# The cross branch's projection computed as four Strassen pairs behind the pairs of the input projection

## The chip, the cores and the metric

The kernel runs on one core of one Trainium2 chip. The metric is the device time of one execution in microseconds (us); the kernel before was timed in three runs. One more execution was profiled, and the durations below come from it. The five engines are called TensorE (PE in the profile, PEld its weight loads), VectorE (DVE), ScalarE (ACT), GpSimd (POOL) and SyncE (SP); SP, ACT and POOL also issue DMA transfers. Each engine executes its own instructions in program order, and waits for other engines through semaphores.

## The reference

One layer of a decoder trunk for 1024 prompt tokens and 8 sample tokens (1032 columns in all), width 1024, in float32. What matters here:

```python
proj = h @ w_in                     # one input projection: q, k, v, gates, u, merge, ...
br_gla = o * jax.nn.silu(gla_g)     # branch 0: gated linear attention
br_pool = p * jax.nn.silu(pool_g)   # branch 1: multi-scale pooling
br_x = c * jax.nn.silu(xg)          # branch 2: cross attention
bproj = einsum('btnw,nwd->btnd', stack([br_gla, br_pool, br_x]), w_branch)
gates = jax.nn.sigmoid(merge)       # one gate per branch and channel
merged = sum(gates * bproj, axis=branch)
y = x + merged @ w_out              # then a final RMSNorm
```

So each of the three branches, 1024 channels by 1032 columns, is multiplied by its own 1024 by 1024 matrix, gated, and summed into one array.

## The kernel before

**Precision.** A float32 value is split into a high half, rounded (ScalarE copy), and the rest (VectorE subtraction), and a product is three matmuls: high by high, high by low and low by high (`split`, lines 221 and 222; `mm3`, lines 240 to 242).

**Input projection.** It runs as 40 *pairs* (class `Pair`). A pair produces 256 output channels for all 1032 columns by one level of Strassen's scheme in Winograd's form: seven products of halves instead of eight. `RIGHT` names the right-hand operands of the products, `11`, `21`, `t2`, `t1`, `t3`, `22`, `t4`: quarters of the input and sums of quarters, 512 channels by 516 columns each. They are split once and stay in SBUF, in 28 tiles of 1032 columns, for all pairs. The left-hand ones (`a11`, `a12`, `s2`, `s1`, `s3`, `s4`, `a22`) are quarters of the pair's weights and sums of them, built anew for each pair by VectorE (`operands`, line 301) and split. One product is 24 matmuls of 258 columns (three per 128 channels of the sum and half of the columns). ScalarE copies partial results out of PSUM (line 612), VectorE adds them (lines 677, 694 and 703).

**Order.** `seq` lists the products: 0 to 4 of a pair, then product 0 of the next pair, then 5 and 6. I write (i, j) for product j of pair i. The weights of a product are prepared three products ahead (`AHEAD`). TensorE's and SP's instructions stand in the order in which the code emits them; those of VectorE, ScalarE and GpSimd are put in order by a scheduler when the kernel is built. Into the pairs a stream of other work is woven (attention, then pooling), which ends before pair 36. Pairs 28 to 39 are *gated*: their result goes through SiLU, is multiplied by a branch's value (`mix`) and stored as the branch's array `br_scr`. Pairs 16 to 27 give the merge gates `m_scr`.

**Branch projection, direct.** After the last pair come 24 *units*: three branches in the order of `ORDER` (cross, GLA, pool), eight blocks of 128 output channels each. `branch_k` loads and splits a branch's array (16 tiles); a unit is 72 matmuls, 24 each for three column blocks of 384, 384 and 264. The result is multiplied by the sigmoid of the merge gate (line 1508), added to the sum so far (line 1510) and stored in `acc_scr`. The output projection follows.

**Buffers.** Wide tiles: `E`, 30 of 1032 columns. Ring tiles: `R`, 15 of 512 columns. Weight halves: `W2`, 8. Raw weights: `RAW`, 3. PSUM: six banks `px` for the products. A load into a wide tile has to wait until the tile's last reader is done.

Of the kernel before, what the change touches and what calls it, by code (L numbers as in the profile page):

```python
# [18 lines left out]
P = 128  # L19
D = 1024  # L20
T = 1024
NS = 8
# [20 lines left out]
EW = 1032  # L43
EXP_LN_SET = 6
# [3 lines left out]
def trunk_kernel(ctx: ExitStack, tc: tile.TileContext,  # L48
# [65 lines left out]
    def R(shape, dt=F32, name="r"):  # L114

        return shaped(wk.tile([P, 512], dt, tag="ring", name=name, bufs=NR), shape)

    def V(shape, dt=F32, name="v"):
        return shaped(wk.tile([P, 512], dt, tag="own", name=name, bufs=4), shape)
# [68 lines left out]
    brs = [cp.tile([P, NK, NS], F32, name=f"brs{n}") for n in range(3)]  # L188
# [13 lines left out]
    acc_scr = [scratch(NK, f"acc{n}_", (P, TT)) for n in range(2)]  # L202
# [78 lines left out]
    ORDER = (2, 0, 1)  # L281

    class Pair:


        def __init__(self, src, dst, s0=None, gated=None, turned=False):
            self.src, self.dst, self.s0, self.gated, self.raw = src, dst, s0, gated, [None, None]
            self.turned = turned
# [300 lines left out]
    def operand(name, k, src):  # L589
        hi, lo = (E([2, HT], F32R, name=f"o{name}{k}{j}") for j in range(2))  # L590
        split(hi, lo, src)
        ops.setdefault(name, []).append((hi, lo))
# [12 lines left out]
    def run_product(n):  # L605
# [18 lines left out]
        def finish(t, e):  # L624
# [3 lines left out]
            if p.gated:  # L628
# [11 lines left out]
                nc.vector.tensor_tensor(t[:, :, 512:HT], t[:, :, 512:HT], ss, op=ALU.mult)  # L640
            if p.turned:
# [24 lines left out]

        if j == 0:
# [13 lines left out]
        elif j == 2:  # L681
            p.r2 = []
            for c in product(p.x, n, False):
                p.r2.append(saved(p.x, c, "r2"))
                yield
# [5 lines left out]
        elif j == 4:  # L691
            for c in product(p.x, n, False):
# [6 lines left out]
        elif j == 5:  # L699
            p.e2 = E([2, HT], name="c2")  # L700
            mixed(1)
            for c in product(p.z, n, False):
# [4 lines left out]
        else:  # L707
            for c in product(p.x, n, False):
# [92 lines left out]
    def cross_scaled(h):  # L801
        xs = wk.tile([P, 16], F32, tag="xsq", name="xsq", bufs=2).rearrange("p (i b) -> p i b", i=2)
# [528 lines left out]
    def emit(n, ahead=AHEAD):  # L1331
        prepare(n + ahead)
        if seq[n] == (28, 0):
# [102 lines left out]
    units = [(o, n, d) for o, n in enumerate(ORDER) for d in range(NK)]  # L1436
    inputs = {}

    def fetch(u):
# [10 lines left out]
        acc = None  # L1450
        if o > 0:
            acc = E([TT], name="acc")
            nc.sync.dma_start(out=acc, in_=acc_scr[o - 1][d])
        inputs[u] = w, sig, acc
# [3 lines left out]
    for n in range(5, len(seq)):  # L1458
        for _ in range({7: 2, 5: 1, 4: 1, 3: 1, 2: 1, 1: 1}.get(len(seq) - n, 0)):
            br.append(branch_k(ORDER[0], len(br)))  # L1460
# [3 lines left out]
    br.append(branch_k(ORDER[0], 7))  # L1464
# [29 lines left out]
    for u, (o, n, d) in enumerate(units):  # L1494
        if d == 0 and o:
# [3 lines left out]
        w, sig, acc = inputs.pop(u)  # L1499
        act(sig, sig, AF.Sigmoid)  # L1500
        ts = [PX() for _ in CH]
# [4 lines left out]
        for t, (c0, cw) in zip(ts, CH):  # L1506
            cs = slice(c0, c0 + cw)
            nc.vector.tensor_tensor(sig[:, cs], t[:, :cw], sig[:, cs], op=ALU.mult)
            if o > 0:
                nc.vector.tensor_tensor(sig[:, cs], acc[:, cs], sig[:, cs], op=ALU.add)  # L1510
        if o < 2:
            nc.gpsimd.dma_start(out=acc_scr[o][d], in_=sig)
# [43 lines left out]
    for hf, order in enumerate(ORDERS):  # L1556
        for tb in order:
# [13 lines left out]
            if hf == 0:  # L1571
                x = (E([D], name="y") if tb < 8 else RAW("ys").rearrange("p a b -> p (a b)"))[:m]
                nc.sync.dma_start(out=x, in_=x_p[tb * P:(tb + 1) * P] if tb < 8 else x_s)
                rows_[tb], sums[tb] = x, wk.tile([P, 4], F32, tag="yq", name="yq", bufs=9)[:m]
# [69 lines left out]
```

## Time and profile before

| | us |
|---|---|
| median of three runs (lowest, highest) | 1431.19 (1431.14, 1432.55) |
| the profiled execution | 1428.62 |
| its span, first to last instruction | 1426.9 |
| TensorE busy | 1403.6 (98%) |
| VectorE busy | 919.8 (64%) |
| ScalarE busy | 678.3 (48%) |
| direct branch projection, first matmul to the output projection's first | 1054.40 to 1326.37 |

The profiled execution is 2.57 us, 0.18%, below the median of the runs; 1.7 us of it lie outside the span. A window row gives, for a stretch of the span, each engine's busy time with its number of instructions, TensorE's granted clock, the share of the 16 DMA engines and the traffic. A timeline row gives start, duration, engine, line, operation and, in brackets, the idle time before it and what ended it. Matmuls overlap, so the busy time of one is longer than the distance to the next.

### The profile page before, as it was taken

How to read it: one execution, taken by the hardware profiler on the slowest of the kernel's cores; microseconds unless marked ns; L12 is line 12 of the kernel's file. 1: busy time of each engine (PE TensorE's matmuls, PEld its weight loads, DVE VectorE, ACT ScalarE, POOL GpSimd, SP SyncE). 2: the span in 40 equal slices, each digit the busy share in tenths (PEclk: the TensorE clock that was granted, in tenths of full speed). 3: DMA queues.
4: the chain of work that ended last, by engine and by line, in shares of the span. 5: the costliest groups of instructions: out<-in, count | busy, mean ns of one | idle time of the engine just before them, and what ended most of it. 6: DMA issues, size and time to landing. Idle time of an engine off the chain costs nothing.

```text
span 1426.9 us, 28403 instructions
## 1 busy us (share of the span) xinstructions
PE 1403.6 (98%) x10625; PEld 1345.0 (94%) x10625; DVE 919.8 (64%) x2108; ACT 678.3 (48%) x1582; POOL 293.6 (21%) x529
## 2 busy tenths in 40 slices
PE   7999999999899999999999999999999999999998
PEld 6899999999899999999999999999999999999876
DVE  6956766857687777767765777876662534654336
ACT  6744434534566656656554545444472422333222
POOL 4154222336442222222221111110000000000000
PEclk9999999999999999999999999999999999999999
DMA  9367786877564565545444556476484687632633
GB/s 347 117 202 248 251 280 208 258 222 237 138 190 130 170 192 163 165 152 166 155 150 146 176 162 210 150 217 204 150 263 148 225 273 232 228 105 86 227 112 117
DMA packets 194197, 270.05 MB, mean 189 GB/s; under 512 B 24252, under 2 KB 144084, under 8 KB 194052
## 3 DMA queue, kind: packets, MB, share of 16 engines
q1 hardware_dynamic: 129692, 151.36, 34.1%
q0 software_dynamic: 26208, 78.94, 15.5%
q10 hardware_dynamic: 38160, 37.95, 9.6%
q8 instruction: 83, 1.36, 0.4%
q14 instruction: 54, 0.44, 0.1%
HBM read 185.84 MB, written 82.80 MB: 188 GB/s over the span
## 4 chain that ended last, share of the span: by engine, by line
PE 92%; DMA 4%; DVE 3%; ACT 1%; issue 1%; SPq 0%; POOL 0%; ACTq 0%; DVEq 0%
PE px L240 26%; PE px L241 26%; PE px L242 26%; PE pz L241 2%; PE pz L242 2%; PE pz L240 2%; DMA raw<-in_w_in_dram 2%; PE pz L461 1%; PE pz L1040 1%; PE pz L1019 1%; DMA qb<-xqs 1%; PE pz L867 1%; PE pz L1021 1%; DMA pT<-pts 0%; PE pz L1126 0%
## 5 line engine op out<-in xcount | busy, mean ns | idle before, releaser
L240 PE MATMUL px<-bh,wbh 128*128 128x384 f32 (+1 forms) x576 | 184.3, 320 | 0.0
L241 PE MATMUL px<-bl,wbh 128*128 128x384 f32 (+1 forms) x576 | 184.0, 319 | 0.0
L242 PE MATMUL px<-bh,wbl 128*128 128x384 f32 (+1 forms) x576 | 183.8, 319 | 0.0
L612 ACT ACTIVATE r<-px 128x258 f32<-128x258 f32 x240 | 90.1, 377 | 54.4 <-PE px L242 53.5
L241 PEld LDWEIGHTS px<-bl,wbh 128*128 128x128 f32 x576 | 108.3, 188 | 0.0
L242 PEld LDWEIGHTS px<-bh,wbl 128*128 128x128 f32 x576 | 108.3, 188 | 0.0
L240 PEld LDWEIGHTS px<-bh,wbh 128*128 128x128 f32 x576 | 108.3, 188 | 0.0
L240 PE MATMUL px<-o,a12h 128*128 128x258 f32 x320 | 92.0, 288 | 1.4 <-DVE c L703 1.4
L240 PE MATMUL px<-ot,s1h 128*128 128x258 f32 x320 | 93.3, 292 | 0.0
L240 PE MATMUL px<-o,s4h 128*128 128x258 f32 x320 | 92.3, 288 | 0.3 <-DVE c L694 0.3
L240 PE MATMUL px<-o,a11h 128*128 128x258 f32 x320 | 92.4, 289 | 0.0
L240 PE MATMUL px<-ot,s2h 128*128 128x258 f32 x320 | 92.3, 288 | 0.0
L240 PE MATMUL px<-ot,a22h 128*128 128x258 f32 x320 | 92.0, 288 | 0.0
L240 PE MATMUL px<-ot,s3h 128*128 128x258 f32 x320 | 91.9, 287 | 0.0
L241 PE MATMUL px<-ot,s2h 128*128 128x258 f32 x320 | 90.6, 283 | 0.5 <-DVE ot L222 0.5
L241 PE MATMUL px<-o,a11h 128*128 128x258 f32 x320 | 90.7, 283 | 0.3 <-DVE o L222 0.3
L241 PE MATMUL px<-o,s4h 128*128 128x258 f32 x320 | 90.7, 283 | 0.0
L242 PE MATMUL px<-o,a11l 128*128 128x258 f32 x320 | 90.7, 283 | 0.0
L242 PE MATMUL px<-o,s4l 128*128 128x258 f32 x320 | 90.7, 283 | 0.0
L242 PE MATMUL px<-ot,s3l 128*128 128x258 f32 x320 | 90.5, 283 | 0.0
L241 PE MATMUL px<-ot,a22h 128*128 128x258 f32 x320 | 90.4, 283 | 0.0
L242 PE MATMUL px<-ot,s1l 128*128 128x258 f32 x320 | 90.4, 282 | 0.0
(479 smaller groups left out, 4687.2 us busy)
## 6 DMA issues: line engine op xcount, KB each, us to landing
raw<-in_w_in_dram ACTq DMA_DIRECT2D x72, 512.0 KB, 4.1
msc<-c POOLq DMA_DIRECT2D x24, 516.0 KB, 4.6
brsc<-c POOLq DMA_DIRECT2D x24, 516.0 KB, 4.1
sig<-msc SPq DMA_DIRECT2D x24, 516.0 KB, 6.1
brr<-brsc SPq DMA_DIRECT2D x48, 256.0 KB, 5.5
wbr<-in_w_branch_dram SPq DMA_DIRECT2D x24, 512.0 KB, 5.9
acc<-sig POOLq DMA_DIRECT2D x16, 516.0 KB, 5.4
acc<-acc SPq DMA_DIRECT2D x16, 516.0 KB, 7.2
```

What stands on the lines that cost most here:

```text
L240: nc.tensor.matmul(out, lhsT=lh, rhs=rh, start=start, stop=False, skip_group_check=more)
L241: nc.tensor.matmul(out, lhsT=lh, rhs=rl, start=False, stop=False, skip_group_check=more)
L242: nc.tensor.matmul(out, lhsT=ll, rhs=rh, start=False, stop=stop, skip_group_check=more)
L461: nc.tensor.matmul(t[:, :DV], lhsT=memT[k // 2][:, k % 2, a * P:(a + 1) * P], rhs=raw[k // 2][:, k % 2], start=k == 0, stop=k == NK - 1)
L612: nc.scalar.activation(r, acc[c][:, :QT], AF.Copy)
L867: nc.tensor.matmul(t[32 * j:32 * j + 32, :DV], lhsT=pm[:, a, 4 * i + j, :], rhs=vc[j][:, a, :], start=a == 0, stop=a == 1)
L1019: nc.tensor.matmul(t[0:64, 0:P], lhsT=ki[:, 0:64], rhs=qi, start=True, stop=True)
L1021: nc.tensor.transpose(t[:, P:2 * P], kt, ident)
L1040: nc.tensor.matmul(to, lhsT=kiqi[:, 1, cs], rhs=st, start=False, stop=True)
```

## The change

The cross branch leaves the direct units. Its projection becomes four more pairs, 40 to 43, behind the input projection's, with the same seven products. Their right-hand operands are the quarters of the cross branch's array and the sums `t1` to `t4` of quarters, in the wide tiles that the input's operands leave free, one after the other. The exchange is spread over pairs 37 to 40 by a table of steps (`turnover`): quarters 12, 11, 22 and 21 are loaded as 16 blocks of 516 columns into ring and own tiles; 16 VectorE subtractions (line 623) turn them into `t1`, `t3`, `t2` and `t4`; the quarters 11, 21 and 22 are loaded once more, whole, into wide tiles; all are split.

Around it: one ungated pair (merge gates of GLA, its last quarter) is taken out of place 27 and put last, at 39, so the gated pairs are 27 to 38; `ORDER` becomes cross, pool, GLA; a branch pair loads two merge gate rows per half, takes their sigmoid and multiplies by them (line 717); 16 direct units are left, all of which add to a sum. Ring and own tiles grow from 512 to 516 columns. The pool branch's sample columns and the sums of the final norm move into the tile `smp`, and one small tile has one buffer instead of two.

```diff
+NBR = 1
...
-    ORDER = (2, 0, 1)
+    ORDER = (2, 1, 0)
...
+    pairs.append(pairs.pop(27))
+    for o, n in enumerate(ORDER[:NBR]):
+        pairs += [Pair(w_branch[n][:, 2 * P * j:2 * P * (j + 1)], acc_scr[o][j], branch=(o, n, j)) for j in range(4)]
     NPAIR = len(pairs)
+    TURNS = {39 + 4 * o: ORDER[o] for o in range(NBR)}
...
+    def block_loaded(n, name, alloc):
+        r, c = int(name[0]) - 1, int(name[1]) - 1
+        turn[name] = [loaded(br_scr[n][2 * r + k // 2][:, 2 * (k % 2) + c], [HT], "b" + name, alloc) for k in range(4)]
+
+    def operand_loaded(n, name):
+        r, c = int(name[0]) - 1, int(name[1]) - 1
+        turn["x", name] = [loaded(br_scr[n][2 * r + k][:, c:4:2], [2, HT], "x" + name, E) for k in range(2)]
+
+    def operand_split(v, name):
+        for x in turn.pop(("x", name)):
+            wide = not isinstance(x, list)
+            hi = E([2, HT], F32R, name=f"v{name}h")
+            lo = x.bitcast(F32R) if wide else E([2, HT], F32R, name=f"v{name}l")
+            with tc.issue_after(last["hi"].ins), tc.issue_after(last["lo"].ins):
+                for y, h, l in [(x, hi, lo)] if wide else [(x[q], hi[:, q], lo[:, q]) for q in range(2)]:
+                    split(h, l, y)
+            ops.setdefault((v, name), []).append((hi, lo))
+
+    def difference(x, y, out, name):
+        with tc.issue_after(last["lo"].ins):
+            for k in range(4):
+                nc.vector.tensor_tensor(out[k], x[k], y[k], op=ALU.subtract)
+        turn["x", name] = [out[:2], out[2:]]
+
+    def turnover(i, j):
+        for at, n in TURNS.items():
+            v, step = 1 + list(TURNS).index(at), (i - at, j)
+            if step == (-2, 3):
+                block_loaded(n, "12", R)
+                block_loaded(n, "11", R)
+            elif step == (-1, 0):
+                block_loaded(n, "22", R)
+            elif step == (-2, 6):
+                block_loaded(n, "21", V)
+            elif step == (-1, 1):
+                difference(turn["12"], turn["11"], turn["11"], "t1")
...
+            elif step == (-1, 5):
+                operand_loaded(n, "11")
+            elif step == (0, 1):
+                operand_split(v, "11")
...
+            elif step == (1, 2):
+                operand_split(v, "t4")
...
-                hi, lo = ops[RIGHT[j]][k // 2]
+                hi, lo = ops[version(i), RIGHT[j]][k // 2]
...
+            if p.branch:
+                for i, sg in enumerate(p.mix[e]):
+                    nc.vector.tensor_tensor(t[:, i], t[:, i], sg, op=ALU.mult)
...
+        def factors(e):
+
+            if p.branch:
+                o, n, g = p.branch
+                for i in range(2):
+                    row = (0, 3, 1, 2)[2 * e + i]
+                    p.mix[e].append(loaded(m_scr[n][g][:, row], [HT], "sg"))
+
+        def sigmoids(e):
+            if p.branch:
+                for sg in p.mix[e]:
+                    with tc.issue_after(last["hi"].ins):
+                        act(sg, sg, AF.Sigmoid)
...
-    units = [(o, n, d) for o, n in enumerate(ORDER) for d in range(NK)]
+    units = [(o, ORDER[o], d) for o in range(NBR, 3) for d in range(NK)]
```

**TensorE, where pair 39 nears its end.** Rows name the output, the left and the moving operand; `o` and `ot` are the input's operands, `v11h` and `x` the halves of the cross branch's quarter 11. Before, product 4 (`s3`) of the last pair is followed by its product 5 (`s4`):

```order
L240 MATMUL px<-ot_830,s3h 128x258
L241 MATMUL px<-ot_831,s3h 128x258
L242 MATMUL px<-ot_830,s3l 128x258
L240 MATMUL px<-o_932,s4h 128x258
L241 MATMUL px<-o_933,s4h 128x258
L242 MATMUL px<-o_932,s4l 128x258
```

After:

```order
L242 MATMUL px<-ot_821,s3h 128x258
L243 MATMUL px<-ot_822,s3h 128x258
L244 MATMUL px<-ot_821,s3l 128x258
L242 MATMUL px<-v11h,a11h 128x258
L243 MATMUL px<-x_14764,a11h 128x258
L244 MATMUL px<-v11h,a11l 128x258
```

Product 0 of pair 40, on the cross branch, now stands between products 4 and 5 of pair 39.

**VectorE, around products 2 to 4 of pair 38.** Rows that end in 258 take a PSUM result (`px`); `s4l` and `a22l` are low halves of weights; `b11` to `b22` are blocks of the cross branch. Before:

```order
L222 TENSOR_TENSOR s4l_14306<-ws_14162,s4h_14305 128x512
L301 TENSOR_TENSOR ws_14416<-ws_14414,raw_14128 128x512
L222 TENSOR_TENSOR a22l_14340<-raw_13986,a22h_14339 128x512
L694 TENSOR_TENSOR c1_14244<-px_14309,r3_14355 128x258
L222 TENSOR_TENSOR a12l_14379<-raw_14240,a12h_14378 128x512
L694 TENSOR_TENSOR c1_14244<-px_14310,r3_14370 128x258
```

After:

```order
L224 TENSOR_TENSOR s4l_14608<-ws_14448,s4h_14607 128x512
L623 TENSOR_TENSOR b22_14438<-b22_14438,b11_14355 128x516
L623 TENSOR_TENSOR b22_14440<-b22_14440,b11_14357 128x516
L623 TENSOR_TENSOR b22_14442<-b22_14442,b11_14359 128x516
L623 TENSOR_TENSOR b22_14444<-b22_14444,b11_14361 128x516
L224 TENSOR_TENSOR a22l_14646<-raw_14248,a22h_14645 128x512
L787 TENSOR_TENSOR c1_14538<-px_14611,r3_14661 128x258
L712 TENSOR_TENSOR c1_14538<-c1_14538,mix_14613 128x512
L787 TENSOR_TENSOR c1_14538<-px_14612,r3_14676 128x258
```

Four subtractions stand ahead of the weights' `a22l` and of the two sums that read PSUM.

**VectorE, around product 4 of pair 39.** Before, the low halves (`bl2`) of the direct operand of the cross branch are made here:

```order
L222 TENSOR_TENSOR s3l_14769<-ws_14766,s3h_14768 128x512
L677 TENSOR_TENSOR c1_14774<-px_14773,r1_14664 128x258
L222 TENSOR_TENSOR bl2_14803<-brr_14808,bh2_14802 128x512
L222 TENSOR_TENSOR bl2_14803<-brs2_116,bh2_14802 128x2x4
L222 TENSOR_TENSOR s4l_14817<-ws_14668,s4h_14816 128x512
```

After, those of `t2` and of quarter 21 (in place, `x21`):

```order
L224 TENSOR_TENSOR vt2l_14919<-b22_14442,vt2h_14918 128x516
L224 TENSOR_TENSOR vt2l_14919<-b22_14444,vt2h_14918 128x516
L224 TENSOR_TENSOR a22l_14925<-raw_14534,a22h_14924 128x512
L787 TENSOR_TENSOR c1_14812<-px_14886,r3_14940 128x258
L787 TENSOR_TENSOR c1_14812<-px_14887,r3_14955 128x258
L224 TENSOR_TENSOR x21_14877<-x21_14877,v21h_14959 128x1032
L224 TENSOR_TENSOR x21_14879<-x21_14879,v21h_14962 128x1032
```

The two sums of pair 39 that free PSUM for its product 5 stand behind four splits of `t2`, and the splits of quarter 21 behind the sums. The direct operands that are split at the end of the pairs are now those of the pool branch, in pair 43.

More of the change, by code (lines that the diff above doesn't have):

```diff
@@ L114, in R @@
     def R(shape, dt=F32, name="r"):
-        return shaped(wk.tile([P, 512], dt, tag="ring", name=name, bufs=NR), shape)
+        return shaped(wk.tile([P, HT], dt, tag="ring", name=name, bufs=NR), shape)
     def V(shape, dt=F32, name="v"):
-        return shaped(wk.tile([P, 512], dt, tag="own", name=name, bufs=4), shape)
+        return shaped(wk.tile([P, HT], dt, tag="own", name=name, bufs=4), shape)
     def WS(shape, name="ws"):
@@ L187, in trunk_kernel @@
     smp = cp.tile([P, 32 * NS], F32, name="smp")
-    brs = [cp.tile([P, NK, NS], F32, name=f"brs{n}") for n in range(3)]
+    brs = [cp.tile([P, NK, NS], F32, name=f"brs{n}") if n != 1 else smp[:, :NK * NS].rearrange("p (k b) -> p k b", k=NK)
+           for n in range(3)]
     als = cp.tile([P, NS], F32, name="als")
@@ L595, in product, with version @@
+    def version(i):
+        return pairs[i].branch[0] + 1 if pairs[i].branch else 0
     def product(acc, n, start):
@@ L1449, in fetch @@
         nc.sync.dma_start(out=sig.rearrange("p (h t) -> p h t", h=2), in_=m_scr[n][d // 2][:, 2 * (d % 2):2 * (d % 2) + 2])
[L1450 to L1454, printed above, removed]
+        acc = E([TT], name="acc")
+        nc.sync.dma_start(out=acc.rearrange("p (h t) -> p h t", h=2),
+                          in_=acc_scr[o - 1][d // 2][:, 2 * (d % 2):2 * (d % 2) + 2])
+        more = [loaded(acc_scr[0][d // 2][:, 2 * (d % 2) + q], [HT], "acm") for q in range(2)] if NBR == 2 else []
+        inputs[u] = w, sig, acc, more
     br = []
@@ L1463, in trunk_kernel @@
         emit(n)
-    br.append(branch_k(ORDER[0], 7))
+        turnover(*seq[n])
+    br.append(branch_k(ORDER[NBR], 7))
     mg, late = [None] * NK, []
@@ L1494, in trunk_kernel @@
     for u, (o, n, d) in enumerate(units):
[L1495 removed]
+        if d == 0 and o > NBR:
             br = [branch_k(n, k) for k in range(NK)]
@@ L1498, in trunk_kernel @@
             fetch(u + 1)
-        w, sig, acc = inputs.pop(u)
+        w, sig, acc, more = inputs.pop(u)
         act(sig, sig, AF.Sigmoid)
+        for q, x in enumerate(more):
+            nc.vector.tensor_tensor(acc[:, q * HT:(q + 1) * HT], acc[:, q * HT:(q + 1) * HT], x, op=ALU.add)
         ts = [PX() for _ in CH]
@@ L1508, in trunk_kernel @@
             nc.vector.tensor_tensor(sig[:, cs], t[:, :cw], sig[:, cs], op=ALU.mult)
-            if o > 0:
-                nc.vector.tensor_tensor(sig[:, cs], acc[:, cs], sig[:, cs], op=ALU.add)
+            nc.vector.tensor_tensor(sig[:, cs], acc[:, cs], sig[:, cs], op=ALU.add)
         if o < 2:
-            nc.gpsimd.dma_start(out=acc_scr[o][d], in_=sig)
+            nc.gpsimd.dma_start(out=acc_scr[o][d // 2][:, 2 * (d % 2):2 * (d % 2) + 2],
+                                in_=sig.rearrange("p (h t) -> p h t", h=2))
         else:
@@ L1573, in trunk_kernel @@
                 nc.sync.dma_start(out=x, in_=x_p[tb * P:(tb + 1) * P] if tb < 8 else x_s)
-                rows_[tb], sums[tb] = x, wk.tile([P, 4], F32, tag="yq", name="yq", bufs=9)[:m]
+                rows_[tb], sums[tb] = x, smp[:m, 64 + 4 * tb:68 + 4 * tb]
             x, sq = rows_[tb], sums[tb]
```

39 lines of the change are left out of this document (32 added, 7 removed).

## The prediction

> **What bounds the kernel now.** I read the busy shares first, then the chain of work that ended last.
>
> ```profile
> PE 1403.6 (98%) x10625; PEld 1345.0 (94%) x10625; DVE 919.8 (64%) x2108; ACT 678.3 (48%) x1582; POOL 293.6 (21%) x529
> PE 92%; DMA 4%; DVE 3%; ACT 1%; issue 1%; SPq 0%; POOL 0%; ACTq 0%; DVEq 0%
> ```
>
> TensorE is busy 98% of the span and carries 92% of the chain. A busy TensorE isn't a full one, since matmuls overlap, so I read its pace from starts in the timeline: product 0 (`a11`) of three successive pairs after the woven-in work has ended, the first direct matmul, the first one of the output projection, and the one place near the change where TensorE waits.
>
> ```profile
> 987.62 0.28 PE L240 MATMUL px<-o,a11h 128*128 128x258 f32 x1
> 1007.78 0.28 PE L240 MATMUL px<-o,a11h 128*128 128x258 f32 x1
> 1027.94 0.28 PE L240 MATMUL px<-o,a11h 128*128 128x258 f32 x1
> 1048.10 0.28 PE L240 MATMUL px<-o,s4h 128*128 128x258 f32 x1
> 1049.98 0.39 PE L240 MATMUL px<-o,s4h 128*128 128x258 f32 x1 [0.29 <-DVE c L694]
> 1051.53 0.28 PE L240 MATMUL px<-ot,a22h 128*128 128x258 f32 x1
> 1054.40 0.34 PE L240 MATMUL px<-bh,wbh 128*128 128x384 f32 x1
> 1326.37 0.39 PE L240 MATMUL px<-woh,mg0h 128*128 128x512 f32 x1
> ```
>
> A pair takes 20.16 us, twice the same: 168 matmuls at 0.120 us, a product of 24 in 2.88 us. The 24 direct units take 1326.37 - 1054.40 = 271.97 us, so one branch takes 90.66 us. Neither stage has slack on TensorE to give; the only loss is in the last pair, where `s4` lasts 3.43 us instead of 2.88, 0.55 us, because its second half waits for a VectorE sum of the product just before it.
>
> **The main term.** Eight units leave, four pairs come: 4 x 20.16 = 80.64 us against 90.66, so **-10.02 us**. In matmuls it is 672 of 258 columns for 576 of mean 344: an eighth fewer columns, but 96 more instructions.
>
> Each matmul brings its own weight load (the same count in both columns above), so I check that 96 more loads cost nothing:
>
> ```profile
> core 0: us, PE busy (x) PEld busy (x) DVE busy (x) ACT busy (x) POOL busy (x), PEclk, DMA share, GB/s
> 983.00:1003.00 20.00, 20.00 (x169) 20.00 (x169) 12.21 (x24) 8.72 (x18) 1.28 (x2) 1.00 0.52 159
> 1043.00:1054.40 11.40, 11.11 (x92) 10.90 (x91) 8.07 (x19) 10.13 (x19) 0.00 (x0) 1.00 0.96 297
> L241 PEld LDWEIGHTS px<-bl,wbh 128*128 128x128 f32 x576 | 108.3, 188 | 0.0
> ```
>
> 169 loads of 188 ns would be 31.8 us end to end and fit into 20.0, so they run under the matmuls, and the pitch of 0.120 us contains them. The granted clock is 1.00 in both rows. The Trainium skill, "TensorE: Matmul & The Clock Gate", section "Part 3: Packing small matmuls — row/col tiling", says that a weight load overlaps a running matmul only when it goes to other row groups; these fill all 128 rows, so by that page the 96 extra loads would come on top. The rows above speak against it.
>
> **The turn, where operands are exchanged.** VectorE gets new work here, in a place where half of its time is already spoken for, so the question is whether it keeps up. Its prices:
>
> ```profile
> 994.14 0.69 DVE L222 TENSOR_TENSOR s1l<-ws,s1h 128x512 fp32r<-128x512 f32 x1
> 994.75 0.68 DVE L638 TENSOR_TENSOR c<-c,mix 128x512 f32<-128x512 f32 x1
> 995.35 0.68 DVE L301 TENSOR_TENSOR ws<-raw 128x512 f32<-128x512 f32 x1
> 998.22 0.16 DVE L640 TENSOR_TENSOR c<-c,brs 128x8 f32<-128x8 f32 x1
> 998.30 0.42 DVE L677 TENSOR_TENSOR c<-px,r 128x258 f32<-128x258 f32 x1
> 1032.98 0.42 DVE L703 TENSOR_TENSOR c<-px,r 128x258 f32<-128x258 f32 x1
> 1033.32 0.68 DVE L222 TENSOR_TENSOR bl<-brr,bh 128x512 fp32r<-128x512 f32 x1
> L222 DVE TENSOR_TENSOR o<-h,o 128x1032 fp32r<-128x1032 f32 x6 | 7.3, 1229 | 1.2 <-ACT o L221 1.2
> ```
>
> In a queue an instruction starts 0.08 us before the one ahead of it is reported done: start to start 0.60 us for 512 columns (0.69 long), 0.34 for 258 (0.42), 0.08 for the small ones (0.16), and so 1.15 for 1032 (1.23). I count 516 columns as 512.
>
> New in the turn are 16 subtractions, 16 split differences of 516 and 6 splits of 1032: 32 x 0.60 + 6 x 1.15 = 26.1 us. I take the clock from the start of (38, 1); a product is 2.88 us. The first VectorE row of the turn, the sum of (38, 1), can start after half a product, at 1.44. The tightest deadline I find is the low half `s4l` of (40, 5), the 20th product from there, due at 19 x 2.88 = 54.7 us: behind it in VectorE's queue stands the sum of (40, 4), which (40, 5) needs as well. Up to `s4l` the queue holds 82 rows: 28 of 512, 32 of 516, 14 of 258, 6 of 1032 and 2 small: 60 x 0.60 + 14 x 0.34 + 6 x 1.15 + 2 x 0.08 = 47.8 us. From 1.44 on that ends at 49.3: **5.4 us to spare**, 90% full. An earlier point, the sums of (39, 4), due at 34.6 for (39, 5): 53 rows, 39 x 0.60 + 10 x 0.34 + 2 x 1.15 + 0.2 = 29.3 us, done at 30.7, 3.9 to spare.
>
> From the spare time go VectorE's own waits. What the wide loads and weight loads cost:
>
> ```profile
> raw<-in_w_in_dram ACTq DMA_DIRECT2D x72, 512.0 KB, 4.1
> msc<-c POOLq DMA_DIRECT2D x24, 516.0 KB, 4.6
> sig<-msc SPq DMA_DIRECT2D x24, 516.0 KB, 6.1
> 1000.98 0.69 DVE L301 TENSOR_TENSOR ws<-raw 128x512 f32<-128x512 f32 x1 [0.36 <-DMA raw<-in_w_in_dram]
> DMA to landing us min/median/max: 3.3/5.7/11.2
> ```
>
> (The last row is that of the 516 KB loads of `sig`.) Quarter 11's tiles come free within (39, 0), near 13.4 us; 6.1 us later it is there, and its splits are queued near 23.7: covered by 4 us. Quarter 21's come free within (39, 1), near 22.2, landed by 28.3, split near 32: covered by 4. Quarter 22 is the tight one: its first tile is the result tile of pair 39, which must be summed (33.4 in VectorE's queue) and stored (4.6) first; issued near 38.5 it lands at 44.6, when VectorE reaches its splits at 46. The second half of each pair's weights already makes VectorE wait 0.36 us today, and in pair 39 it shares the DMA engines with quarter 21, so I give it 1 to 2 us. Followed through in order, I count 2.7 us of waits up to `s4l`, which leaves about 2.7 us. So most likely TensorE doesn't stall in the turn; a small stall of **+0.5 us** is what I take between 0 and the bounds: if every row took its whole duration (0.69, 0.42, 1.23, 0.16) the 82 rows were 55.0 us and, with 2.7 us of waits from 1.44 on, 4.4 us too late; if quarter 22 took the longest landing, 11.2, it would be 5.1 late, 2.4 of it uncovered.
>
> The Trainium skill, "VectorE: DVE Perf Modes", section "The DRAIN you can't avoid", says that the next VectorE instruction doesn't start until the pipe of the one before has emptied; read as whole durations that is the 4.4 us above. The starts 994.14, 994.75 and 995.35 show 0.60, not 0.69.
>
> ScalarE has 16 halves of 516 and 6 of 1032 more in the turn. Its busy time is 8.72 us of a pair's 20, and its 512-wide halves are 0.63 long:
>
> ```profile
> L221 ACT ACTIVATE a22h<-raw 128x512 fp32r<-128x512 f32 x2 | 1.3, 632 | 3.9 <-PE px L241 3.9
> L75 ACT ACTIVATE sig<-sig 128x1032 f32<-128x1032 f32 x24 | 25.5, 1063 | 34.2 <-DMA sig<-msc 34.0
> L75 ACT ACT_TABLE_LOAD x4 | 5.1, 1283 | 0.1
> ```
>
> 16 x 0.63 + 6 x 1.06 = 16.4 us in 55 us, on top of 24: 74% full, hidden. If that cover were gone it would show as VectorE waiting for high halves, inside the bounds above. Of the function tables, the sigmoid is loaded once in pair 40.
>
> **What costs nothing.** The branch pairs' four multiplies (4 x 0.60 us) stand where a gated pair has them, in a VectorE 12.21 of 20 busy. Gating begins one pair earlier, at 27, which puts the same 2.6 us into a pair of
>
> ```profile
> 700.00:800.00 100.00, 100.00 (x837) 97.73 (x836) 65.32 (x153) 48.09 (x116) 19.97 (x37) 1.00 0.50 155
> ```
>
> 65% VectorE. Stores of the sum go out on POOL as before, eight of 516 KB for eight. SP's queue holds the 16 block loads from pair 35 on, each behind a free ring tile; the `mix` loads queued behind them are issued a product or more before they are used. TensorE's order is unchanged up to (39, 4). The 0.55 us loss at the last pair moves to pair 43, which again has no next pair between `s3` and `s4`: 0 by it, between -0.55 and +0.5. Wider ring tiles, the moved small tiles and the swapped `ORDER` add no instruction.
>
> **Sum.** 1428.62 - 10.02 + 0.5 = 1419.1 us for the profiled execution. That one is 2.57 below the median of the runs, so against the median: 1431.19 - 9.5 = **1421.7 us**.
>
> **The rivals.**
> *VectorE binds in the turn.* Either bound above, or both: 2.5 to 7 us of TensorE idle between (39, 5) and (41, 1). For it: 90% full, in-order, many hand-overs. Against: rows are closer than their durations. Time 1424 to 1428.5.
> *The gain is eaten up.* The stall of both bounds (6.8 us) and as much again in pairs 40 to 43, since sums arrive late for several products: 7 to 13 us, no change, 1428.5 to 1434. Against: a branch pair needs VectorE 12 us of 20, so it catches up within one.
> *Slower, by weight loads landing late.* VectorE takes the second half of a pair's weights in order, and everything else queues behind it. In pairs 38 to 40 the six wide loads (3.2 MB in 46 us, 69 GB/s) come on top of 159 GB/s. If that made the weights of five pairs land 9.4 us after issue instead of 4.1, each would cost 5.3 - 2.7 = 2.6 us, 13 us in all: 1434 or more. It decides from 6.8 us on, where the spare time ends. For it: single loads up to 11.2. Against: 297 GB/s were moved from 1043 to 1054 with 0.29 us of waiting.
> *Slower, by weight loads that aren't hidden.* 96 x 0.188 = 18.0 us more, 1431.19 - 10.02 + 18.0 = 1439. It contradicts 169 loads in 20.0 us. By the page named with that row this is what would happen.
>
> **How the numbers follow.** Forecast 76%; VectorE binds 14%; eaten up 4%; weights late 5%; loads not hidden 1%. Low end: no stall, no loss at the last pair, and 0.4 for the spread of medians: 1420.2. High end: the whole first bound, 1421.2 + 4.4, and 0.8 of the second: 1426.4. About 0.2%, 2.9 us, is what a measurement can tell from no change. Faster by more needs a stall below 7.2 us: 76 + most of 14, 88%. Same 6%, slower 6%.
>
> **What would show it.** Starts of `a11h` in pairs 40 to 43 20.16 us apart, and the direct stage 181.3 us long: main term. In the timeline between (39, 5) and (41, 1) no TensorE idle over 0.5 us, with VectorE near 90% busy there: the turn. TensorE waiting for an `s4l` or `x22` row or for a sum of line 787: VectorE binds. VectorE waiting for `raw` by more than 2 us per pair: weights late. I'd be wrong if pairs 40 to 43 ran at another pitch than 0.120 us with nothing to wait for.

## The result, and the profile after the change

The changed kernel takes 1421.78 us (median of 13 executions, 1418.5 to 1429.23); the kernel before took 1430.5 us in the 13 executions taken beside it. The ratio is 0.9947, 95% interval 0.9933 to 0.9962: 8.7 us less. The forecast was 1421.7 us, 9.5 us less.

The profiled execution happens to be the slowest of the 13, 1429.23 us, so its span hardly differs from the span before, and I read stages instead of spans. Busy shares of the page, after the change:

```profile
PE 1399.7 (98%) x10721; PEld 1340.6 (94%) x10721; DVE 958.6 (67%) x2166; ACT 697.5 (49%) x1630; POOL 296.5 (21%) x529
```

The 96 matmuls more, with 96 weight loads, take less time in all. The timeline of TensorE (start, length in us, then line, tiles and shape; what it waited for in brackets), with the start of product `a11` of pairs 39 to 43, the two places where product 5 starts late, the first direct matmul and the first one of the output projection:

```profile
1037.17 0.28 PE L242 MATMUL px<-o,a11h 128*128 128x258 f32 x1
1057.32 0.28 PE L242 MATMUL px<-v11h,a11h 128*128 128x258 f32 x1
1061.28 0.39 PE L242 MATMUL px<-o,s4h 128*128 128x258 f32 x1 [0.95 <-DVE c L787]
1078.77 0.29 PE L242 MATMUL px<-v11h,a11h 128*128 128x258 f32 x1
1098.92 0.29 PE L242 MATMUL px<-v11h,a11h 128*128 128x258 f32 x1
1119.08 0.29 PE L242 MATMUL px<-v11h,a11h 128*128 128x258 f32 x1
1139.50 0.39 PE L242 MATMUL px<-v22h,s4h 128*128 128x258 f32 x1
1145.47 0.34 PE L242 MATMUL px<-bh,wbh 128*128 128x384 f32 x1
1326.79 0.39 PE L242 MATMUL px<-woh,mg0h 128*128 128x512 f32 x1
```

From `a11` of pair 39 to the first matmul of the output projection it is 1326.79 - 1037.17 = 289.62 us, where it was 1326.37 - 1027.94 = 298.43 before: **8.81 us less**, the whole gain. Pairs 41 to 43 start 20.15 and 20.16 us apart, the 16 direct units take 181.32 us. One interval is longer: from `a11` of pair 40 to that of pair 41, 1057.32 to 1078.77, it is 21.45 us. These **1.30 us** are lost in the turn, where product 5 of pair 39 (`s4`) waits for the sums of its product 4 (line 787). That wait is what the experiments are about.

What the profiled execution lost, it lost far ahead of the change. `a11` of pair 36, before and after:

```profile
967.48 0.28 PE L240 MATMUL px<-o,a11h 128*128 128x258 f32 x1
```

```profile
976.73 0.28 PE L242 MATMUL px<-o,a11h 128*128 128x258 f32 x1
```

It is 9.25 us later after the change, in a part whose work is all but the same (one gated pair stands there in place of the ungated one that was moved). The table by stretches of 10 us (busy times by engine, then the granted clock, the DMA share and GB/s) shows, of all stretches ahead of it, one with a clock clearly below 1 before:

```profile
360.00:370.00 10.00, 6.55 (x40) 6.14 (x39) 3.60 (x6) 2.83 (x6) 6.72 (x11) 0.83 0.56 153
```

and three after:

```profile
160.00:170.00 10.00, 10.00 (x80) 9.28 (x79) 6.95 (x14) 5.69 (x12) 4.31 (x7) 0.84 0.45 118
220.00:230.00 10.00, 7.14 (x41) 7.14 (x42) 7.22 (x18) 4.48 (x13) 3.26 (x7) 0.66 0.45 130
370.00:380.00 10.00, 8.15 (x43) 7.96 (x44) 3.60 (x8) 2.72 (x6) 6.74 (x11) 0.66 0.71 164
```

The missing clock is 10 x (0.16 + 0.34 + 0.34) = 8.4 us against 10 x 0.17 = 1.7 us, 6.7 of the 9.25 us. Longer waits of TensorE in the same places come with it. Near 223 us, after the change, it waits for a VectorE row `ps`:

```profile
222.86 0.35 PE L953 MATMUL pz<-ident,ps 8*128 8x8 f32 x2 [3.73 <-DVE ps L942]
```

The same wait before:

```profile
217.03 0.26 PE L858 MATMUL pz<-ident,ps 8*128 8x8 f32 x2 [0.85 <-DVE ps L847]
```

Near 158 us it is 2.41 us against 1.63. The stretches of low clock overlap with such waits, so the two losses can't simply be added. All of this lies in the attention stage. In the profiles of the experiments between 1.7 and 10 us of clock are missing ahead of pair 36, and a further execution of the unaltered changed kernel (below) lost 1.7. So the stage times below are compared from `a11` of pair 39 on, and not the spans; there the granted clock is 1.00, except behind the long waits of experiments 8, 10 and 11.

### The profile page after: what moved, and what is told of

Same layout as the page of the kernel before. It is cut to its first block, busy times and chain, and to the rows that moved or that the text cites. A ratio compares the mean times of both kernels' runs of the same rounds, so it can differ in the third digit from the quotient of the medians.

```text
span 1427.5 us, 28722 instructions
## 1 busy us (share of the span) xinstructions
PE 1399.7 (98%) x10721; PEld 1340.6 (94%) x10721; DVE 958.6 (67%) x2166; ACT 697.5 (49%) x1630; POOL 296.5 (21%) x529
## 4 chain that ended last, share of the span: by engine, by line
PE 52%; DVE 2%; DMA 2%; ACT 1%; issue 0%; DVEq 0%
PE px L242 16%; PE px L243 16%; PE px L244 16%; PE pz L242 1%; PE pz L244 1%; PE pz L243 1%; DMA raw<-in_w_branch_dram 1%; DVE b L623 1%; DMA raw<-in_w_in_dram 1%; DMA out_dram<-s 0%; PE px L1662 0%; PE pz L1135 0%; PE pz L1368 0%; PE pz L1114 0%; DVE ws L303 0%
## 5 line engine op out<-in xcount | busy, mean ns | idle before, releaser
L686 ACT ACTIVATE r<-px 128x258 f32<-128x258 f32 x264 | 99.0, 377 | 57.0 <-PE px L244 54.2
L244 PE MATMUL px<-bh,wbl 128*128 128x384 f32 (+1 forms) x384 | 122.8, 320 | 0.0
L243 PE MATMUL px<-bl,wbh 128*128 128x384 f32 (+1 forms) x384 | 122.7, 319 | 0.0
L242 PE MATMUL px<-bh,wbh 128*128 128x384 f32 (+1 forms) x384 | 122.7, 319 | 0.0
L242 PE MATMUL px<-ot,s3h 128*128 128x258 f32 x320 | 92.7, 290 | 1.0 <-ACT r L686 1.0
L242 PE MATMUL px<-ot,s1h 128*128 128x258 f32 x320 | 93.4, 292 | 0.0
L243 PE MATMUL px<-ot,s3h 128*128 128x258 f32 x320 | 90.9, 284 | 0.0
L243 PE MATMUL px<-ot,s1h 128*128 128x258 f32 x320 | 90.5, 283 | 0.0
L244 PE MATMUL px<-ot,a22l 128*128 128x258 f32 x320 | 90.4, 283 | 0.0
```

The source lines that it names most:

```text
L242: nc.tensor.matmul(out, lhsT=lh, rhs=rh, start=start, stop=False, skip_group_check=more)
L243: nc.tensor.matmul(out, lhsT=lh, rhs=rl, start=False, stop=False, skip_group_check=more)
L244: nc.tensor.matmul(out, lhsT=ll, rhs=rh, start=False, stop=stop, skip_group_check=more)
L686: nc.scalar.activation(r, acc[c][:, :QT], AF.Copy)
```

## The experiments

Two figures are read from each profile: the interval between `a11` of pairs 40 and 41 (20.16 us without a stall) and the time from `a11` of pair 39 to the output projection ("in all"). Experiments 1, 5, 10 and 12 were timed in four to six executions; each of the others was executed once, so only its stage times are read.

What VectorE does ahead of the late sums, in the changed kernel: its timeline, from the four subtractions of difference `t2` (line 623, printed as one row) to the sums of line 787, of pair 38 first and then of pair 39:

```profile
1034.43 2.50 DVE L623 TENSOR_TENSOR b<-b,b 128x516 f32<-128x516 f32 x4
1037.46 0.41 DVE L787 TENSOR_TENSOR c<-px,r 128x258 f32<-128x258 f32 x1
...
1052.00 0.69 DVE L224 TENSOR_TENSOR a11l<-raw,a11h 128x512 fp32r<-128x512 f32 x1
1056.56 0.69 DVE L303 TENSOR_TENSOR ws<-raw 128x512 f32<-128x512 f32 x1 [3.87 <-DMA raw<-in_w_branch_dram]
1057.17 0.69 DVE L224 TENSOR_TENSOR s4l<-ws,s4h 128x512 fp32r<-128x512 f32 x1
1057.77 2.51 DVE L224 TENSOR_TENSOR vt2l<-b,vt2h 128x516 fp32r<-128x516 f32 x4
1060.20 0.69 DVE L224 TENSOR_TENSOR a22l<-raw,a22h 128x512 fp32r<-128x512 f32 x1
1060.80 0.76 DVE L787 TENSOR_TENSOR c<-px,r 128x258 f32<-128x258 f32 x2
```

and all of its waits between the start of product 1 of pair 38 and these sums (us in all, times, longest):

```profile
DVE ws L303 <- DMA raw<-in_w_branch_dram: 3.9, 1, 3.9
DVE s3l L224 <- ACT s3h L223: 1.0, 1, 1.0
DVE s2l L224 <- ACT s2h L223: 0.4, 1, 0.4
```

The large wait is for the second half of pair 40's weights. These are the issues around it, on ScalarE's, GpSimd's and SP's queues:

```profile
1047.97 0.37 ACTq L294 DMA_DIRECT2D raw<-in_w_branch_dram  x1
```

```profile
1047.87 0.56 POOL L728 DMA_DIRECT2D brsc<-c  x1 [5.31 <-issue]
```

```profile
1048.05 1.17 SPq L823 DMA_DIRECT2D x<-brsc  x2
```

```profile
1050.20:1056.30 6.10, 6.10 (x53) 6.10 (x53) 2.49 (x3) 4.65 (x10) 0.00 (x0) 1.00 0.85 323
```

The weights, a store of pair 39 and the two loads of quarter 21 are issued within 0.9 us, 2.1 MB together; the DMA engines then move 323 GB/s for 6.1 us at 0.85 busy, and VectorE is released 8.6 us after the weights' issue. The other halves of weights issued near it landed in 3.4 and 3.5 us. The issue itself is late: 10.80 us after `a11` of pair 39, where in pair 37 of the kernel before it was 996.48 - 987.62 = 8.86.

The Trainium skill, "DMA: Bandwidth & Descriptors", section "Issuing engines are not separate DMA queues", says that transfers started by different engines run on the same 16 DMA engines and interleave. These rows agree: issued on three queues, the store, the weights and the two loads land 7.4, 8.6, 8.8 and 9.5 us after their issue, in a spread of 2.1 us.

Two theories follow. **Collision**: the weights are late since they share the DMA engines with quarter 21. **VectorE**: its queue is too full ahead of these sums, and the wait on the weights covers time that would be lost anyway.

### 1: the weights ahead of quarter 21

```
     with tc.issue_after(last["hi"].ins):
-        pairs[i + 1].load(j // 4, nc.scalar)
+        pairs[i + 1].load(j // 4, nc.sync if (i, j) == (39, 4) else nc.scalar)
```

> The second half of pair 40's weights is issued on SP's queue ahead of quarter 21's two loads, not on ScalarE's queue 0.1 us ahead of them. Collision theory (four transfers issued within 0.9 us, the weights land 8.6 us after issue): the weights have landed when VectorE comes to their difference, its wait falls from 3.87 us to under 0.5, the sum of line 787 is ready in time, and product a11 of pairs 40 and 41 start 20.16 to 20.3 us apart, not 21.45: TensorE gains 1.1 to 1.3 us. VectorE theory (its queue is too full ahead of the sums of (39, 4), the wait on the weights covers work that would take that time anyway): the wait shrinks but TensorE still waits 0.5 us or more for line 787, 20.7 to 21.5 us.

Measured: 1422.46 us, ratio 0.9923 (0.9906 to 0.9940), not to be told from the changed kernel; 21.54 us between `a11` of pairs 40 and 41, 289.73 us in all. Both theories missed, since the edit didn't do what I meant. SP's queue and VectorE's in this run:

```profile
1045.49 0.39 SPq L294 DMA_DIRECT2D raw<-in_w_branch_dram  x1
```

```profile
1044.73 0.68 DVE L303 TENSOR_TENSOR ws<-raw 128x512 f32<-128x512 f32 x1
...
1052.81 0.69 DVE L303 TENSOR_TENSOR ws<-raw 128x512 f32<-128x512 f32 x1 [2.64 <-DMA raw<-in_w_branch_dram]
...
1057.05 0.42 DVE L787 TENSOR_TENSOR c<-px,r 128x258 f32<-128x258 f32 x1
1057.38 2.37 DVE L224 TENSOR_TENSOR x<-x,v21h 128x1032 fp32r<-128x1032 f32 x2
1059.67 0.42 DVE L787 TENSOR_TENSOR c<-px,r 128x258 f32<-128x258 f32 x1
```

The load lands in a tile that the difference at 1044.73 still has to read, so it was issued only when that was done, 10.83 us after `a11` of pair 39, as late as before, and collided again. And the order of VectorE's queue changed by itself: the two splits of quarter 21 now stand between the two sums, 2.37 us, which takes back what the shorter wait (2.64) gave. So the place of these two splits in the queue was worth as much here as the earlier landing.

### 2: quarter 21 later

```
-    operand_loaded(n, "21")
+    operand_loaded(n, "21", nc.scalar)
```

> Quarter 21's two loads go to ScalarE's queue, behind the second half of pair 40's weights and ScalarE's next few instructions, some 2.5 to 3.5 us later than now. Collision theory: the weights, alone with one store, land within 4 to 5.5 us of issue instead of 8.6, VectorE waits under 1 us for them, and product a11 of pairs 40 and 41 start 20.16 to 20.4 us apart; quarter 21 lands near the time of its splits, which may cost VectorE up to 2 us later with no stall of TensorE over 0.3 us. VectorE theory: 20.7 to 21.5 us as now.

Measured: 20.13 us, 288.36 us in all, and TensorE has no wait between 950 and 1200 us. VectorE:

```profile
1050.37 0.69 DVE L303 TENSOR_TENSOR ws<-raw 128x512 f32<-128x512 f32 x1 [2.12 <-DMA raw<-in_w_branch_dram]
```

The loads went out 3.8 us behind the weights (1047.34 against 1043.53). The stall is gone, as the collision theory has it; the size isn't as expected, the weights still took 6.8 us and VectorE waited 2.1 us, not under 1. During those 3.8 us only one other transfer was on its way, the store of pair 39, issued 0.1 us ahead of the weights. So of the 5.1 us by which the weights were late in the changed kernel (8.6 against 3.5), quarter 21 accounts for 1.8; the other 3.3 stand beside the store, which no run moves.

### 3: without the subtractions

```
     for k in range(4):
-        nc.vector.tensor_tensor(out[k], x[k], y[k], op=ALU.subtract)
+        pass
```

> Leaves out the 16 subtractions of the turn (the blocks are split as they were loaded), 9.6 us of VectorE's queue in pairs 38 and 39; all loads, splits and matmuls stay. VectorE theory: TensorE's wait for line 787 goes, a11 of pairs 40 and 41 20.16 to 20.2 us apart, and VectorE has idle time ahead of every split. Collision alone, with the queue's lateness no part of it: the weights' half is issued at the usual 8.9 us after a11 of pair 39 (10.8 now), but its transfer still shares the DMA engines with quarter 21's, which don't depend on VectorE; it lands 6 us or more after issue and the wait of VectorE for it stays over 2 us. If both are needed (late issue and collision), the landing is 4.5 to 6 us after issue and there is no stall.

Measured: 20.15 us, 288.27 us in all, no wait of TensorE. The weights' half is issued 8.85 us after `a11` of pair 39 (1040.21 - 1031.36), and VectorE takes it without waiting:

```profile
1046.31 0.69 DVE L303 TENSOR_TENSOR ws<-raw 128x512 f32<-128x512 f32 x1
```

So it landed within 6.1 us, with quarter 21's loads issued as long after `a11` as before, 10.9 us, and now 2.0 us behind it. VectorE comes to this row hardly earlier than in the changed kernel, 14.95 us after `a11` of pair 39 against 15.5 (1056.56 - 3.87 - 1037.17), so it is the load that came in time, not the shorter queue at this row. It takes **both**: VectorE's own lateness delays the issue by 2 us, and the transfer then meets quarter 21's in full. With quarter 21 later (experiment 2) or the issue on time (here) there is no stall.

### 4: the changed kernel once more

> The changed kernel once more, unaltered, to see whether the stall of the turn is the same in each execution. In three profiles of the same instructions VectorE's wait for the second half of pair 40's weights less the stall came to 2.57 (3.87 - 1.30, 3.08 - 0.51). If the stall is what the load's landing leaves over: again the wait less 2.57, between 0 and 1.5 us. If it were fixed by VectorE's queue: 1.3 us whatever the wait.

Measured: 21.09 us, a stall of 0.94 us, with a wait of 3.53 us for the weights; 289.25 us in all. In the run with two branches (5, below) the same instructions of the first turn gave a wait of 3.08 and a stall of 0.51. The stall is the wait less 2.6 (3.87 - 1.30 and 3.08 - 0.51 give 2.57, 3.53 - 0.94 gives 2.59), and 2.12 us in experiment 2 give none. So it isn't one number: it changes from one execution to the next with the landing of one load, 0.5 to 1.3 us in the three seen.

### 5: a second branch as pairs

```
-NBR = 1
+NBR = 2
```

> A second branch (the pooled one) as Strassen pairs too, with a second turn over pairs 41 to 44; 8 direct units stay, each with one more sum to load and two more additions. My count: another -10.02 us for the main term, and the second turn stalls 1 to 3 us like the first, since the same four transfers meet and the loads of the merge gates come on top: 1421.8 - 10.0 + 1 to 3 = 1413 to 1415 us. VectorE theory: the second turn also carries the branch multiplies and stalls over 5 us: 1417 or more.

Measured: 1416.45 us, ratio 0.9878 (0.9858 to 0.9898); 279.84 us from pair 39 to the output projection, 9.8 less than the changed kernel's 289.62. The second turn cost 0.79 + 0.50 us (20.94 and 20.65 between `a11` of pairs 44, 45 and 46) and the first 0.51. The main term comes a second time in full. With the branch multiplies on top the second turn lost 1.29 us in all, within the 0.5 to 1.3 seen in the first, and far from the 5 us of the VectorE theory. The time itself is above the 1413 to 1415 expected, but the kernel before was slower beside these executions too, 1433.1 us; 0.9878 of 1430.5 would be 1413.

### 6: the gated pair last

```
-    pairs.append(pairs.pop(27))
...
-        if seq[n] == (27, 0):
+        if seq[n] == (28, 0):
```

> The pairs of the cross branch stay, but pair 27 isn't moved: the last pair of the input projection is a gated one, and its gating (four multiplies of 512 columns and two small ones, 2.6 us of VectorE by start-to-start) falls into the turn. Theory (the turn is late by VectorE's queue and by the weights that collide with quarter 21): two of the multiplies come behind the second sum of pair 39, in front of splits that are due; stall between the starts of a11 of pairs 40 and 41 grows from 0.5-1.3 us to 2-4 us. Rival (the move is worth nothing, the queue has room): the same 0.5 to 1.3 us.

Measured: 21.71 and 21.34 us after `a11` of pairs 40 and 41, 291.07 us in all. TensorE's waits:

```profile
PE px L242 <- DVE c L786: 1.0, 2, 0.6
PE px L244 <- DVE s1l L224: 0.5, 1, 0.5
```

(Line 786 is 787 here.) Besides the place seen so far TensorE now waits in the next interval as well; 2.75 us are lost in all. Only 1.56 of them fall between `a11` of pairs 40 and 41, less than the 2 to 4 expected there, and more than the rival's 0.5 to 1.3. VectorE waits differently here, 1.7 us for the weights and 1.7 for ScalarE's `v11h`. Against the 289.25 to 289.62 us of the changed kernel, the move of pair 27 is worth 1.5 to 1.8 us, read from single executions.

### 7: the move alone

```
+    pairs.append(pairs.pop(27))
     NPAIR = len(pairs)
...
-        if seq[n] == (28, 0):
+        if seq[n] == (27, 0):
```

> The kernel before with the one edit that an ungated pair stands last in the input projection; no branch runs as pairs. My prediction gave it nothing: pairs 20.16 us apart once the woven-in work has ended, the last pair again some 0.5 us long, the direct stage 272 us, so from a11 of pair 39 to the first matmul of the output projection 298.4 us as before, within 0.3. Rival (the ungated pair last is worth something by itself, since the direct stage's first operands are split beside it): 297.9 or less, the 0.55 us of the last pair gone.

Measured on the kernel before: 298.64 us (298.43 without the move), 0.49 us in the last pair (0.55). Alone it changes nothing, as predicted; it earns its 1.5 to 1.8 us only beside the turn.

### 8: twice the work for VectorE

```
         nc.vector.tensor_tensor(out[k], x[k], y[k], op=ALU.subtract)
+        nc.vector.tensor_tensor(out[k], out[k], out[k], op=ALU.max)
```

> Quarter 21's loads on ScalarE's queue as in the run that had no stall, and behind each of the 16 subtractions one more VectorE instruction of the same shape that changes nothing (the maximum of a block with itself), 16 x 0.60 = 9.6 us more. It measures the room that VectorE's queue has in the turn. By the changed kernel's profile s2l of pair 39 was written 3.3 us before its product, so 9.6 us more should stall TensorE 5 to 7 us in all between a11 of pairs 38 and 41. If VectorE had the 5.4 us to spare that I counted up to the end of the turn and made up the rest in its waits: 3 to 5 us. If a few us of queue don't matter at all: under 1 us.

Measured: 26.85 us between `a11` of pairs 39 and 40 and 20.60 to the next, 7.15 us lost, just over the 5 to 7 expected; 295.48 us in all, where experiment 2, with quarter 21's loads in the same place, had 288.36. TensorE's longest wait is for the sums of pair **38**'s product 4 (line 787, here 788):

```profile
1038.12 0.56 PE L242 MATMUL px<-o,s4h 128*128 128x258 f32 x1 [5.08 <-DVE c L788]
```

Ahead of these sums stand 12 of the 16 added rows, 0.605 us each from start to start, 7.3 us; the product starts 5.24 us late (1038.12, due 2.88 after `a11` of pair 39 at 1030.00). VectorE's room at that point is 2.0 us, less than at any that I had worked out. Not all of the loss is the late start. Behind the wait the clock is low (the last three figures are granted clock, DMA share and GB/s):

```profile
1038.10:1040.00 1.90, 1.88 (x9) 1.90 (x10) 1.90 (x4) 0.91 (x2) 0.00 (x0) 0.50 0.60 169
```

For some 3 us matmuls start 0.215 us apart instead of 0.120. That is 26.85 - 20.15 - 5.24 = 1.46 us of the loss; 0.45 more is lost in the next pair.

### 9: the subtractions on GpSimd

```
-        nc.vector.tensor_tensor(out[k], x[k], y[k], op=ALU.subtract)
+        nc.gpsimd.tensor_tensor(out[k], x[k], y[k], op=ALU.subtract)
```

> The 16 subtractions of the turn go from VectorE to GpSimd. Nearest row: a GpSimd sum of 128x256 takes 0.73 us, so 1.4 to 1.5 us each, 23 us on an engine that is otherwise 6% busy there; VectorE's queue gets 9.6 us shorter as in the run without them. If that is all, the weights' half is issued on time and TensorE doesn't stall: a11 of pairs 40 and 41 20.15 to 20.2 us apart. Rival (GpSimd's work holds up what is queued behind it, the stores of pairs 38 and 39, and so quarters 11 and 22): VectorE or ScalarE waits for those loads, 1 to 5 us of stall in pairs 39 to 41.

Measured: 20.16 us, 288.25 us in all, no stall, as without the subtractions. They take 1.31 to 1.83 us each, and GpSimd, with nothing else in front, makes them between 973 and 1017 us, in pairs 36 to 38, ahead of the place that they had on VectorE (pairs 38 and 39). VectorE slows down beside them, GpSimd's row first:

```profile
1010.18 6.78 POOL L623 TENSOR_TENSOR b<-b,b 128x516 f32<-128x516 f32 x4 [6.00 <-DMA b<-brsc]
```

```profile
1012.64 1.45 DVE L303 TENSOR_TENSOR ws<-raw,ws 128x512 f32<-128x512 f32 x1
1014.01 0.42 DVE L797 TENSOR_TENSOR c<-px,r 128x258 f32<-128x258 f32 x1
1014.35 1.45 DVE L224 TENSOR_TENSOR s1l<-ws,s1h 128x512 fp32r<-128x512 f32 x1
1015.72 1.78 DVE L712 TENSOR_TENSOR c<-c,mix 128x512 f32<-128x512 f32 x1
```

Rows with two SBUF operands that took 0.69 take 1.45 to 1.78 beside a subtraction, while the sum that reads one operand from PSUM keeps its 0.42. Here VectorE has the time.

### 10 and 11: two branches, both turns on GpSimd

> Two branches as pairs, the subtractions of both turns on GpSimd. Two branches with VectorE's subtractions lost 0.5 us in the first turn and 1.3 us in the second; one branch with GpSimd's lost nothing. By the queue theory (what stalls is VectorE's lateness, which its own subtractions start): first turn 0, second 0 to 0.5, since the branch multiplies of pairs 42 and 43 stay on VectorE; from a11 of pair 39 to the output projection 278.3 to 278.8 us against 279.84, and 1.5 us less than with VectorE's, 0.985 to 0.988 of the kernel before. Rival (in the second turn GpSimd's subtractions hold up the stores of the branch pairs behind them, or VectorE's rows stretch while GpSimd works): 280 us or more.

Measured: 1420.92 us, ratio 0.9933 (0.9910 to 0.9956), 285.26 us: **5.4 us worse** than with VectorE's subtractions. The first turn loses nothing, but pair 41 takes 27.21 us. GpSimd, VectorE and TensorE there:

```profile
1085.68 7.50 POOL L623 TENSOR_TENSOR b<-b,b 128x516 f32<-128x516 f32 x6
```

```profile
1085.46 8.28 DVE L717 TENSOR_TENSOR c<-c,sg 128x516 f32<-128x516 f32 x1
```

```profile
1094.39 0.58 PE L244 MATMUL px<-vt3h,s3l 128*128 128x258 f32 x1 [4.97 <-DVE s3l L224]
```

One VectorE multiply of two SBUF tiles, elsewhere 0.69 us, lasted 8.28 us: it ended only when GpSimd's six subtractions in a row had. The split `s3l` stands behind it, and TensorE behind that. Of the 7.06 us that pair 41 loses, 4.97 are this wait; most of the rest is clock, 0.50 from 1094.40 to 1098.40 us.

> The run before with quarter 21's loads behind the weights on ScalarE's queue too. If a rest of stall is left by the collision of these loads with the weights it goes: 278.0 to 278.4 us from a11 of pair 39 to the output projection. If the rest is VectorE's own work, the same as without, within 0.2.

Measured: 287.85 us. Pair 41 took 28.68 us, and TensorE waited 6.1 us for a split (`s1l`). The same happened to another row. GpSimd first, then VectorE:

```profile
1080.46 9.97 POOL L623 TENSOR_TENSOR b<-b,b 128x516 f32<-128x516 f32 x8
```

```profile
1080.25 10.74 DVE L224 TENSOR_TENSOR s1l<-ws,s1h 128x512 fp32r<-128x512 f32 x1
```

Eight subtractions in a row, and a split of two SBUF tiles ended only behind them. What quarter 21's place is worth can't be read beside this; the expectation of 278.0 to 278.4 rested on the second turn being free of stalls, and it isn't.

### 12: each turn on the engine that suits it

```
-        nc.vector.tensor_tensor(out[k], x[k], y[k], op=ALU.subtract)
+        (nc.gpsimd if n == ORDER[0] else nc.vector).tensor_tensor(out[k], x[k], y[k], op=ALU.subtract)
```

> Two branches as pairs; the first turn's 16 subtractions on GpSimd, as in the run without a stall, the second turn's on VectorE, where GpSimd's back-to-back subtractions held a VectorE multiply for 8.3 us. If both readings hold: first turn 0 (0.5 with VectorE's), second 1.3 us as with VectorE's, no VectorE instruction of this part over 2 us, and 279.2 to 279.5 us from a11 of pair 39 to the output projection, against 279.84 with all on VectorE: 0.986 to 0.990 of the kernel before. Rival (the first turn's relief only moves the lateness on into pair 41): 279.8 or more.

Measured: 1415.86 us, ratio 0.9873 (0.9854 to 0.9892), 278.28 us from pair 39 on. All intervals between `a11` of pairs 39 to 47 are 20.15 to 20.22 us; the only cost seen is 0.20 us in pair 37, where GpSimd works. It is 1.6 us better there than with VectorE's subtractions (279.84), more than expected, since the second turn lost nothing either. VectorE's order of work up to the sums of the second turn is the same in both, and it came to them 2.1 us earlier here. The traces show where that began. Counted back from `a11` of pair 43, the second half of pair 42's weights was issued 31.5 us ahead here and 30.2 in the run with VectorE's subtractions, the store of the sum `acc` behind it 17.4 ahead against 16.1, and in that run VectorE then waited 1.6 us for this store, here not at all. So the lateness of the first turn seems to be handed on to the second; no run was made to test that. In whole times the two can't be told apart, and both beat the changed kernel.

## Why the prediction was right, and where it was off

- **The main term, -10.02 us: right.** Pairs 41 to 43 start 20.15 and 20.16 us apart, and pair 40 is longer by the stall alone; the direct stage takes 181.32 us (forecast 181.3). From pair 39 on the account closes: -10.02 + 1.30 (turn) + 0.49 - 0.55 (last pair) = -8.78, measured -8.81.
- **The weight loads: hidden, as the rows said.** 96 loads more left the pitch at 0.120 us, so the rule on row groups in the Trainium skill, "TensorE: Matmul & The Clock Gate", section "Part 3: Packing small matmuls — row/col tiling", which would have made it 1439 us, doesn't hold for these matmuls. The same section of the Trainium skill also lets a load into a background weight buffer go ahead, which I had left out.
- **VectorE's prices: right.** Four subtractions of 516 columns take 2.50 us, so (2.50 - 0.68) / 3 = 0.61 from start to start, not 0.69; the 4.4 us that whole durations would have cost are not there. The sentence of the Trainium skill that I set beside that figure ("VectorE: DVE Perf Modes", section "The DRAIN you can't avoid") is followed there by another: an instruction that isn't held back by the ones before it starts earlier. The rows agree with that one.
- **The stall, +0.5: the step that was mis-sized.** I gave VectorE 2.7 us of waits, 1 to 2 of them for the weights that share the DMA engines with quarter 21. The weights' wait alone was 3.87, 3.08 and 3.53 us. And I set the waits against the 5.4 us to spare at the end of the turn, not against the 3.9 (34.56 - 30.74, so rather 3.8) at the sums of (39, 4), which I had worked out in the sentence after. In the trace of the changed kernel, counted from the start of (38, 1) at 1025.65, the first of the 53 rows starts at 2.05 instead of 1.44, behind the wait of 0.98 us for `s3h`, which so lies ahead of the rows that I counted. The rows take 29.5 us (29.3 were counted), the waits among them 3.87 + 0.36 = 4.2, and they end at 35.8 where 34.6 was due: 1.2 us late, and TensorE loses 1.30. In the other two executions the wait is 0.79 and 0.34 us shorter, and the stall 0.79 and 0.36. The rows of the queue were counted right; the waits, and the point, were wrong.
- **The tightest point was another one.** (38, 4) has 2.0 us of room (experiment 8); I looked from (39, 4) on. In the changed kernel nothing used up these 2.0 us, so it cost nothing.
- **Quarter 22, which I called tight, cost nothing:** VectorE splits it at 1074.28 us without a wait, and from pair 41 on a branch pair starts every 20.15 us.
- **The mark that I named for "VectorE binds"**, TensorE waiting for a sum of line 787, did appear, at 0.5 to 1.3 us and not the 2.5 to 7 that I gave this rival. Its mechanism is real and lies 2 to 3 us of VectorE work away, as experiments 6 and 8 show.
- **The mark of "weights late"**, VectorE waiting more than 2 us for `raw`, appeared twice, in pair 39 (3.87 us) and in pair 41 (4.06, ahead of the row of line 303 at 1097.48). The second cost TensorE nothing (20.15 us from `a11` of pair 41 to the next): what a wait costs depends on the room where it falls. As a cause of its own, at 13 us over five pairs, the rival didn't come.
- **What costs nothing:** the move of pair 27 alone, yes (298.64 against 298.43). That it costs nothing beside the turn was too little said: there it saves 1.5 to 1.8 us.
- **The sum.** 9.5 us were forecast, 8.7 measured. That the time itself, 1421.78, agrees with 1421.7 to a tenth is partly luck: the stall was 0.4 to 0.8 us larger in two of three profiles, and the kernel before came out 0.7 us lower in more executions than in the three that I had.

## What to carry to other kernels

Set an engine's waits against the room at each deadline along its queue, not only against the room at the end; here 3.8 us of room at one point met 4.2 us of waits, in a queue that began 0.6 us late. Look for the moment when a new load goes out beside old transfers: four within 0.9 us turned a landing of 3.5 us into 8.6, and moving two of them by 3.8 us brought it to 6.8, which was enough to remove the stall. And moving work to an idle engine helps only where the busy one can afford its interference: the same 16 subtractions on GpSimd took the stall away in one turn and cost 7 us in the next, where they came in a row.

## What the hardware showed that I had not expected

**VectorE held by GpSimd for six instructions, and for eight.** The multiply of 8.28 us and the split of 10.74 us above. The Trainium skill, "SBUF — State Buffer", section "Who interferes with whom", says that the two share one pair of ports under an exclusive lock, and that a VectorE instruction with two SBUF inputs contends with a GpSimd instruction that reads SBUF. The rows agree in kind: rows with two SBUF operands stretch from 0.69 to 1.45 or 1.78 us, one with a PSUM operand doesn't. They show more than one instruction's lock: VectorE got no turn between six subtractions of 1.25 us each, nor between eight. That GpSimd is what held it is read from the times; in experiment 12, with the second turn's subtractions on VectorE, no VectorE row of this part is longer than 1.8 us.

**A long wait of TensorE costs clock as well.** Behind the waits of 5 to 6 us in experiments 8, 10 and 11 the granted clock was 0.50, and matmuls came 0.215 us apart instead of 0.120. Ahead of the change, in the attention stage, the stretches of low clock go with waits of TensorE too: of 2.41 and 3.73 us near 158 and 223 us, and of 1.88 and 1.58 in a row near 370. There the same instructions lost 1.7 us of clock in one execution of the changed kernel and 8.4 in another. These 6.7 us are most of the range from 1418.5 to 1429.23 us and three quarters of what the change is worth; the two single profiles, before and after, have spans only 0.6 us apart. No run was made to vary these waits, and the length at which the clock falls isn't shown: before the change, 1.63 us near 158 us left it at 1.00.
